# Dense products on plain float32 operands instead of three sweeps over high and low parts, in a two-layer hybrid backbone

## The chip, the cores and the metric

The kernel runs on 1 core of one Trainium2 chip, as one launch. The metric is the device time of that core in microseconds (us); lower is better. Six things work side by side on the core: TensorE's matmuls (PE in the rows) and its weight loads (PEld), VectorE (DVE), ScalarE (ACT), GpSimd (POOL), and SyncE (SP), which here only issues transfers.

## The reference

Two layers run over 256 latent tokens and 256 context tokens of width 1024. Each layer is one wide input projection, three token mixers (Fourier mixing, a gated delta rule, differential attention), three output projections merged under gates, an output projection, and a squared-ReLU MLP. All arrays are float32.

```
u_f, dn_qkv, dn_z, dn_ab, da_q, da_k, da_v, gates = split_columns(h @ w_in)     # 1024 -> 7184
y_f  = fourier_mix(u_f) @ w_f
y_dn = deltanet_output(o_dn, dn_z, dn_gain, h.dtype) @ w_dn
y_da = diff_output(o_da, da_gain, lam_init) @ w_da
y = gated_merge(y_f, y_dn, y_da, gates) @ w_o
x = x + g1 * y
h2 = rms_norm(x, norm2[l]) * (1 + sc2) + sh2
x = x + g2 * squared_relu_mlp(h2, w_mlp1[l], w_mlp2[l])                          # 1024 -> 4096 -> 1024
```

In layer 0 both streams run through everything, so the products are mostly 512 columns (tokens) wide. In layer 1 only the latent tokens go past the mixers, so most products are 256 columns wide.

## The kernel before, in words

Every weight matrix is cut into chunks of 128 x 1024 floats (512 KB). `load_w` brings one chunk into a ring of four buffers called `raw` (a transfer issued by SP), then ScalarE writes a rounded copy `whi` in float32r (a 32-bit type that TensorE takes in one sweep), and VectorE (GpSimd for some chunks) writes the rest, `wlo` = `raw` - `whi`. The moving side is split in the same way: the modulated input `h` into `hh` and `hl`, the MLP's inner activations into two tiles `a`, the mixers' outputs into `yh`/`yl` and `ydh`/`ydl`; `split` does it with one ScalarE copy and one VectorE subtraction.

`mm3` then makes one 128 x 128 block of a product with three matmuls into the same PSUM bank: high x high, low x high, high x low. `gemm` runs the eight blocks of a chunk; `step_of` runs one block of several chunks while the input is still being made (in the fronts of both layers and at the start of each MLP).

A few products take plain float32 operands before and after the change: the 128 x 128 steps of the delta rule (`state`, `k`, `U`, `vn`, ...), attention scores (`km`, `q`) and values (`aT`, `vt`), and the conditioning vector's product with 384 columns (`wn`, `cT`). The levels of a triangular inverse (`Tm`, `Um`, `C`, `X`) run in float16, 64 columns wide.

The order of work on TensorE is set by priorities. Dense products record their own time in `Weave.account`, and the steps of the delta rule and of attention ("chains") are placed between them at times that are given in the same count: `at(t)` looks up which dense product stands at time t. So what `account` believes of a product's length decides how many dense products stand between two steps of a chain.

The first branch's gated results are written out to HBM (`spill`) and read back into `merged` before the other two branches are added; `merged` is then split into `hh`/`hl` for the output projection.

Of the kernel before, what the change touches and what calls it, by code (L numbers as in the profile page):

```python
# [49 lines left out]
LN2 = math.log(2.0)  # L50
FWD = (2, 3, 0, 1)
# [78 lines left out]

SHIFT = ((0, 48), (80, 0))
PAD = {"y": (48, 0), "yd": (40, 104), "a": ((0, 112), (0, 0))}


def pad(pool, w):
    if w:
        pool.tile([P, w], F32, name="pad")


class Weave:  # L140
# [24 lines left out]
    def transpose(self, out, a, ident):  # L165
        self.pe.transpose(out, a, ident)
        self.account(ident, 4)
# [14 lines left out]
def body(tc, A, dbg=None):  # L182
# [13 lines left out]
    hs = [[], []]  # L196
    for t_, at_ in zip(("hh", "hl"), SHIFT):
        t = hp.tile([P, KT * T + max(at_)], F32R, name=t_)
        for l_ in range(DEPTH):
            hs[l_].append(t[:, at_[l_]:at_[l_] + KT * T].rearrange("p (k c) -> p k c", c=T))  # L200
    wx = ExitStack()

    wp = wx.enter_context(tc.tile_pool(name="wp", bufs=3, reuse_waits="tile"))
# [37 lines left out]
    turn_dn = [0]  # L241

    def load_w(l, n, pair=None, eng=V):
        if l == 1 and n < C_U:

            eng = (G, V)[turn_dn[0] % 2]
            turn_dn[0] += 1
        r = raw_tile(A["wck"][l, n])
        if pair is None:
            hi = wp.tile([P, 1024], F32R, tag="whi", name="whi")  # L250
            lo = wp.tile([P, 1024], F32R, tag="wlo", name="wlo")
        else:
            hi, lo = pair[:, 0], pair[:, 1]
# [15 lines left out]
    def step_of(jobs, k, t0, n, order=range(KT), X=hs[0]):  # L269

        for ps, w, m in jobs:
            mm3(ps[0:m, t0:t0 + n], w[0][:, k], w[1][:, k], X[0][:, k, t0:t0 + n], X[1][:, k, t0:t0 + n], k == order[0], k == order[-1])

    def split(src, hi, lo):
        S.copy(hi, src)  # L275
        V.tensor_tensor(out=lo, in0=src, in1=hi.bitcast(F32), op=ALU.subtract)  # L276
# [65 lines left out]
    def lambdas(pool):  # L342
        raw = wp.tile([P, 1024], F32, tag="raw", name="raw", bufs=4)
# [16 lines left out]
    strir = cst.tile([P, 2, P], F32R, name="strir")  # L360
# [4 lines left out]
    def masks():  # L365
# [3 lines left out]
        r = raw_tile(A["kc"][:, K_STRI:K_STRI + 256], 256)  # L369
        S.copy(strir, r.rearrange("p (a b) -> p a b", a=2))  # L370
# [82 lines left out]
    def modulate(l, x, r, a, base, s, k, pool, eng=V):  # L453
        sl = slice(s * L, (s + 1) * L)
        t = pool.tile([P, L], F32, tag="mt", name="mt", bufs=3)
        hi, lo = hs[l][0][:, k, sl], hs[l][1][:, k, sl]
        gain, shift = a[:, k, s:s + 1], ada[l][:, base + k, s:s + 1]
        V.scalar_tensor_tensor(out=t, in0=x[s][:, k], scalar=gain, in1=r[s], op0=ALU.mult, op1=ALU.mult)
        S.activation(hi, t, AF.Identity, bias=shift)
        if eng is V:  # L460
            V.scalar_tensor_tensor(out=lo, in0=t, scalar=shift, in1=hi.bitcast(F32), op0=ALU.add, op1=ALU.subtract)
        else:
            S.activation(t, t, AF.Identity, bias=shift)
            eng.tensor_tensor(out=lo, in0=t, in1=hi.bitcast(F32), op=ALU.subtract)

    def mixer(l, last, front):
# [3 lines left out]
        H = hs[l]  # L470
# [15 lines left out]
        def product(key, c, m, eng=V):  # L486
            return pre.pop(key) if key in pre else gemm(load_w(l, c, None, eng), H, m)

        def gate_weights():
            w = raw_tile(A["wab"][l].rearrange("p a b -> p (a b)"), 128).rearrange("p (a b) -> p a b", b=16)  # L490
            wab = [wp.tile([P, 8, 16], F32R, tag=f"wab{i}", name=f"wab{i}", bufs=1) for i in range(2)]
            split(w, wab[0], wab[1])
            return wab

        def dn_gates():
# [14 lines left out]
            def rest():  # L510
                with weave.chain() as at:
# [27 lines left out]
                    ghr = mk("ghr", F32R)  # L539
                    V.tensor_copy(ghr, g)  # L540
                    glo = mk("glo")
                    V.tensor_tensor(out=glo, in0=g, in1=ghr.bitcast(F32), op=ALU.subtract)
                    glr = mk("glr", F32R)
                    V.tensor_copy(glr, glo)
                    at(t0 + GATE[1])
                    for d in range(2):
                        gd = g[:, d].rearrange("p a b -> p (a b)")
                        PE.matmul(pc[:, 16 * d:16 * d + 16], tri[d], gd, start=True, stop=True)
                        for i, x_ in enumerate((ghr, glr)):
                            PE.matmul(pc[:, 32 + 16 * d:48 + 16 * d], strir[:, d], x_[:, d].rearrange("p a b -> p (a b)"), start=i == 0, stop=i == 1)  # L550
# [7 lines left out]
                    gates.update(beta=beta, ghi=ghr, glo=glo, neg=neg, bend=bend, eg=ee[:, 0], egl=ee[:, 2], g=g)  # L558
# [90 lines left out]
        def dn_chain(p, q2, k2, ktm, vtm, since, lat):  # L649
# [40 lines left out]
            def prepare(steps, t0):  # L690
# [16 lines left out]
                for i, s in enumerate(steps):  # L707
                    tiles = (FWD[s], BWD[s])
                    rh, rl = quad("rh", F32R), quad("rl", F32R)
                    for u, (d, h) in enumerate(units):  # L710
                        for r_, g_ in ((rh, gates["ghi"].bitcast(F32)), (rl, gates["glo"])):
                            g_ = g_[:, d, s, 2 * p + h:2 * p + h + 1]
                            S.activation(r_[:, u], tri[d], AF.Copy, scale=g_)
# [157 lines left out]
        spill = dram.tile([P, KT, n], F32, name=f"spill{l}")  # L871

        early = {}

        def open_gate(cg, i, eng=V):
            ps = product((cg, i), cg + i, n, eng)
# [4 lines left out]
        def branch(cg, cp, Y, put, side, ahead=2):  # L881

            ths, wpj = {i: early.pop((cg, i)) for i in range(KT) if (cg, i) in early}, None
            for i in range(KT + ahead):
# [9 lines left out]
                V.scalar_tensor_tensor(out=th, in0=th, scalar=1.0, in1=pp_[:, :n], op0=ALU.add, op1=ALU.mult)  # L894
                put(j, th)
                side()

        def fnet():
# [4 lines left out]
            ct = [fp.tile([P, 2 * L], F32R, name=f"ct{i}") for i in range(2)]  # L903
            split(raw_tile(A["ct"], 2 * L), ct[0], ct[1])
            ct = [c_.rearrange("p (k c) -> p k c", k=2) for c_ in ct]
            cc = [fp.tile([P, 256], F32R, name=f"cc{i}") for i in range(2)]
            split(raw_tile(A["kc"][:, K_CC:K_CC + 256], 256), cc[0], cc[1])
# [3 lines left out]
            for c in range(4):  # L911
                w = [w_.rearrange("p k c -> p (k c)") for w_ in load_w(l, C_U + c)]
                for i in range(2):
                    k, cols = 2 * c + i, slice(512 * i, 512 * i + 512)
                    for t in range(nt):
                        tk = slice(t * P, (t + 1) * P)
                        mm3(ps[t], H[0][:, k, tk], H[1][:, k, tk], w[0][:, cols], w[1][:, cols], k == 0, k == KT - 1)
            u = [fp.tile([P, nt, 512], F32R, name=f"u{i}") for i in range(2)]
            for t in range(nt):
                split(ps[t], u[0][:, t], u[1][:, t])  # L920
            units = [(g, s) for g in range(4) for s in range(nseq)]

            def positions(i):

                pq = bank("pg").rearrange("p (a c) -> p a c", a=2)
                for j, (g, s) in enumerate(units[i:i + 2]):
                    gs = slice(g * P, (g + 1) * P)
                    for k in range(2):
                        mm3(pq[:, j], u[0][:, 2 * s + k, gs], u[1][:, 2 * s + k, gs], ct[0][:, k], ct[1][:, k], k == 0, k == 1)
                return pq  # L930

            def channels(i, z):

                pa_, pb_ = (abank()[:, :2 * w_].rearrange("p (a c) -> p a c", a=2) for w_ in (NC + 1, NC - 1))
                mm3(pa_, cc[0][:, 0:P], cc[1][:, 0:P], z[0][:, :, 0:NC + 1], z[1][:, :, 0:NC + 1], True, True)
                mm3(pb_, cc[0][:, P:2 * P], cc[1][:, P:2 * P], z[0][:, :, NC - 1:L], z[1][:, :, NC - 1:L], True, True)

                y = fp.tile([P, 2, L], F32, tag="y", name="y")
                sn = y[:, :, L - 1:NC - 1:-1]
                S.copy(y[:, :, NC:L], pb_[:, :, NC - 2:0:-1])  # L940
# [3 lines left out]
                g = units[i][0]  # L944
                hi, lo = (t[:, g:g + 2] if last else t[:, g].rearrange("p (a c) -> p a c", a=2) for t in yb)
                split(y, hi, lo)
# [566 lines left out]
```

## Time and profile before

| | |
|---|---|
| time, median of 3 runs | 1585.76 us (1582.19 to 1586.18) |
| the profiled execution's own time | 1584.71 us |
| its span, first to last instruction | 1582.6 us |
| TensorE matmuls busy | 1517.0 us (96%), 10114 instructions |
| weight loads busy | 1305.2 us (82%) |
| VectorE / ScalarE / GpSimd busy | 1166.3 / 735.4 / 145.0 us |
| moved from and to HBM | 209.42 MB read, 4.20 MB written |

Busy times overlap between engines, and matmuls overlap each other: a matmul of 512 columns is shown with about 0.39 us, while the next one starts well before it ends. How fast TensorE gets through its work is therefore read from the distance between starts, not from durations.

### The profile page before, as it was taken

What the parts mean: (1) busy time and instruction counts of PE and PEld (TensorE: products, weight loads), DVE (VectorE), ACT (ScalarE), POOL (GpSimd) and SP (SyncE); (2) the same over time, 40 slices, a digit from 0 to 9 for tenths busy, and PEclk for the clock granted to TensorE, in tenths of its full rate; (3) what the DMA queues carried; (4) which work ended last, traced back from release to release, by engine and by line L of the source; (5) the groups of instructions that cost most, each with busy time, mean ns of one, the idle gap of its engine ahead of it and who ended that gap; (6) DMA issues with size and microseconds to landing.
All of it is one profiled execution on the core that took longest, in us unless ns stands there. A gap on an engine that the chain in (4) does not pass through costs nothing. (4 is left out here: it accounts for less than half of the span.)

```text
span 1582.6 us, 26109 instructions
## 1 busy us (share of the span) xinstructions
PE 1517.0 (96%) x10114; PEld 1305.2 (82%) x10114; DVE 1166.3 (74%) x2246; ACT 735.4 (46%) x1527; POOL 145.0 (9%) x173
## 2 busy tenths in 40 slices
PE   5899999999999999999999998899999999999997
PEld 2588888777888878888888888888988899999997
DVE  8787774768789797867676755776777886877765
ACT  3475533676532233423223233575457644555543
POOL 3400100011000012000000004001111100100001
PEclk9999999999999999999999999899999999999998
DMA  7532124211257573566566542141332135655662
GB/s 237 192 97 67 35 75 124 82 48 35 80 187 226 189 237 109 164 193 195 181 196 186 186 148 86 56 150 48 111 103 68 42 106 186 188 175 184 190 185 93
DMA packets 64461, 215.31 MB, mean 136 GB/s; under 512 B 7281, under 2 KB 12305, under 8 KB 64081
## 3 DMA queue, kind: packets, MB, share of 16 engines
q1 hardware_dynamic: 58178, 201.96, 40.7%
q10 hardware_dynamic: 5184, 7.21, 1.4%
q0 software_dynamic: 976, 4.48, 1.0%
q8 instruction: 79, 1.29, 0.4%
q14 instruction: 44, 0.36, 0.1%
HBM read 209.42 MB, written 4.20 MB: 135 GB/s over the span
## 5 line engine op out<-in xcount | busy, mean ns | idle before, releaser
L254 ACT CAST whi<-raw 128x1024 fp32r<-128x1024 f32 x277 | 290.5, 1050 | 220.6 <-PE pg L158 98.5
L255 DVE TENSOR_TENSOR wlo<-raw,whi 128x1024 fp32r<-128x1024 f32 x269 | 329.7, 1226 | 80.1 <-ACT whi L254 71.3
L158 PE MATMUL pg<-hh,whi 128*128 128x512 f32 (+1 forms) x856 | 304.0, 355 | 0.2
L158 PE MATMUL pg<-hh,wlo 128*128 128x512 f32 (+1 forms) x856 | 302.9, 354 | 0.5 <-DVE wlo L255 0.5
L158 PE MATMUL pg<-hl,whi 128*128 128x512 f32 (+1 forms) x856 | 303.1, 354 | 0.0
L336 DVE CUSTOM_DVE_ANT_0 junk<-raw,cb 128x1024 f16<-128x1024 f32 x128 | 157.0, 1227 | 57.8 <-DMA raw<-in_wt 56.3
L158 PEld LDWEIGHTS pg<-hh,whi 128*128 128x128 f32 x856 | 162.7, 190 | 20.6 <-issue 0.8
L158 PEld LDWEIGHTS pg<-hl,whi 128*128 128x128 f32 x856 | 162.8, 190 | 19.5 <-issue 0.8
L158 PEld LDWEIGHTS pg<-hh,wlo 128*128 128x128 f32 x856 | 162.7, 190 | 19.1 <-DVE wlo L255 0.7
L158 PE MATMUL pg<-a,whi 128*128 128x256 f32 (+1 forms) x448 | 107.5, 324 | 0.1
L435 POOL TENSOR_TENSOR acc<-acc,sq 128x256 f32<-128x256 f32 x36 | 38.1, 1067 | 661.7 <-ACT sq L433 661.7
L632 DVE SCALAR_TENSOR_TENSOR cy<-cu,conv,cy 128x512 f32<-128x512 f32 (+1 forms) x96 | 69.3, 723 | 30.3 <-ACT cy L630 29.0
L158 PEld LDWEIGHTS pg<-a,whi 128*128 128x128 f32 x448 | 75.8, 188 | 7.7 <-DVE a L276 0.8
L158 PE MATMUL pg<-a,wlo 128*128 128x256 f32 (+1 forms) x224 | 72.1, 322 | 0.0
L878 ACT ACTIVATE gt<-pg 128x256 f32<-128x256 f32 (+1 forms) x43 | 21.0, 488 | 102.6 <-PE pg L158 99.3
L158 PE MATMUL pd<-a,whi 128*128 128x512 f32 (+1 forms) x224 | 56.7, 334 | 0.1
L158 PE MATMUL pa<-hh,whi 128*128 128x512 f32 (+1 forms) x152 | 54.5, 358 | 1.0 <-ACT cy L630 0.9
L158 PE MATMUL pa<-hh,wlo 128*128 128x512 f32 (+1 forms) x152 | 54.0, 355 | 0.0
L158 PE MATMUL pa<-hl,whi 128*128 128x512 f32 (+1 forms) x152 | 53.6, 353 | 0.0
L1235 DVE TENSOR_TENSOR mr<-mr 128x512 f32<-128x512 f32 (+1 forms) x64 | 35.4, 555 | 23.6 <-ACT mr L1234 23.6
L158 PE MATMUL pg<-whi,hh 128*128 128x256 f32 (+1 forms) x160 | 50.9, 318 | 0.7 <-DVE q L996 0.5
L158 PE MATMUL pg<-wlo,hh 128*128 128x256 f32 (+1 forms) x160 | 50.1, 314 | 0.0
(444 smaller groups left out, 3611.4 us busy)
## 6 DMA issues: line engine op xcount, KB each, us to landing
raw<-in_wck SPq DMA_DIRECT2D x280, 512.0 KB, 3.6
raw<-in_wt SPq DMA_DIRECT2D x80, 512.0 KB, 3.6
wv<-in_wt SPq DMA_DIRECT2D x10, 512.0 KB, 4.1
wn<-in_wn SPq DMA_DIRECT2D x16, 192.0 KB, 3.7
x<-in_xin SPq DMA_DIRECT2D x4, 512.0 KB, 8.2
spill<-gt ACTq DMA_DIRECT2D x8, 256.0 KB, 3.9
cb<-crow POOLq DMA_DIRECT2D x2, 1024.0 KB, 7.0
merged<-spill ACTq DMA_DIRECT2D x8, 256.0 KB, 4.6
```

Of the source, the lines that this page charges most:

```text
L158: ins = self.pe.matmul(out, a, b, start=start, stop=stop)
L254: S.copy(hi, r)
L255: eng.tensor_tensor(out=lo, in0=r, in1=hi.bitcast(F32), op=ALU.subtract)
L336: V.tensor_tensor_reduce(out=junk, in0=r, in1=self.cb[:, v], scale=0.5, scalar=0.0, op0=ALU.mult, op1=ALU.add, accum_out=ada[l][:, n, v:v ...
L435: G.tensor_tensor(out=self.acc[s], in0=self.acc[s], in1=q, op=ALU.add)
L632: V.scalar_tensor_tensor(out=y3, in0=u[:, 0:ns, j:j + L], scalar=conv[:, f, j:j + 1], in1=y3, op0=ALU.mult, op1=ALU.add)
L878: S.activation(th, ps[:, :n], AF.Tanh, scale=0.5)
L1235: V.tensor_tensor(out=t, in0=t, in1=t, op=ALU.mult)
```

## The change

Weights are used straight from `raw`, whose ring grows from 4 to 11 buffers; `whi`, `wlo`, `hl`, the second halves of `a`, `y`, `yd` and the Fourier tiles are gone, and with them every copy and subtraction that made them. Each block of a product is one matmul on float32 operands. `merged` becomes a tile that stays in SBUF from the first branch to the output projection, so the transfers of `spill` and the split of `merged` go. `Weave.account` counts a float32 product as 2 sweeps instead of 4 (an ordering number, no work). In the last MLP the appended column count falls from two to one (258 to 257 columns), and two small float32r pairs (`ghr`/`glr`, `rh`/`rl`) become one float32 product each.

```diff
-    wp = wx.enter_context(tc.tile_pool(name="wp", bufs=3, reuse_waits="tile"))
+    wp = wx.enter_context(tc.tile_pool(name="wp", bufs=1, reuse_waits="tile"))
...
-        self.account(b, 4 if b.dtype == F32 else 1)
+        self.account(b, 2 if b.dtype == F32 else 1)
...
+    H = hp.tile([P, KT, T], F32, name="h")
+    M = hp.tile([P, KT, T], F32, name="merged")
...
-        r = wp.tile([P, 1024], F32, tag="raw", name="raw", bufs=4)
+        r = wp.tile([P, 1024], F32, tag="raw", name="raw", bufs=RAW)
...
-    def load_w(l, n, pair=None, eng=V):
...
-        S.copy(hi, r)
-        eng.tensor_tensor(out=lo, in0=r, in1=hi.bitcast(F32), op=ALU.subtract)
-        return hi.rearrange("p (k c) -> p k c", c=P), lo.rearrange("p (k c) -> p k c", c=P)
-
-    def mm3(ps, wh, wl, xh, xl, first, last):
-        PE.matmul(ps, wh, xh, start=first, stop=False)
-        PE.matmul(ps, wl, xh, start=False, stop=False)
-        PE.matmul(ps, wh, xl, start=False, stop=last)
+    def load_w(l, n, dst=None):
+        if dst is None:
+            dst = raw_tile(A["wck"][l, n])
         else:
+            nc.sync.dma_start(dst, A["wck"][l, n])
+        return dst.rearrange("p (k c) -> p k c", c=P)
 
     def gemm(w, X, n, k0=0, kts=KT, t0=0):
         ps = bank()
         for k in range(kts):
-            mm3(ps[:, :n], w[0][:, k0 + k], w[1][:, k0 + k], X[0][:, k, t0:t0 + n], X[1][:, k, t0:t0 + n], k == 0, k == kts - 1)
+            PE.matmul(ps[:, :n], w[:, k0 + k], X[:, k, t0:t0 + n], start=k == 0, stop=k == kts - 1)
...
-        S.activation(hi, t, AF.Identity, bias=shift)
-        if eng is V:
-            V.scalar_tensor_tensor(out=lo, in0=t, scalar=shift, in1=hi.bitcast(F32), op0=ALU.add, op1=ALU.subtract)
-        else:
-            S.activation(t, t, AF.Identity, bias=shift)
-            eng.tensor_tensor(out=lo, in0=t, in1=hi.bitcast(F32), op=ALU.subtract)
+        S.activation(H[:, k, s * L:(s + 1) * L], t, AF.Identity, bias=ada[l][:, base + k, s:s + 1])
...
-                        for j, r_ in enumerate((rh, rl)):
-                            PE.matmul(pD[:, d * 256:(d + 1) * 256], strir[:, d], flat(r_)[:, d * 256:(d + 1) * 256],
-                                      start=False, stop=d == 1 and j == 1)
+                        PE.matmul(pD[:, d * 256:(d + 1) * 256], stri[:, d], flat(r_)[:, d * 256:(d + 1) * 256], start=False, stop=d == 1)
...
+                dst = M[:, j, :n] if first else th
+                V.scalar_tensor_tensor(out=dst, in0=th, scalar=1.0, in1=pp_[:, :n], op0=ALU.add, op1=ALU.mult)
+                if not first:
+                    V.tensor_tensor(out=M[:, j, :n], in0=M[:, j, :n], in1=th, op=ALU.add)
...
-        M = tp.tile([P, KT, n], F32, name="merged")
-        for j in range(KT):
-            nc.scalar.dma_start(M[:, j], spill[:, j])
...
-        for k in range(KT):
-            split(M[:, k], H[0][:, k, :n], H[1][:, k, :n])
...
-                V.tensor_tensor(out=t, in0=t, in1=t, op=ALU.mult)
-                split(t, a[0][:, j], a[1][:, j])
+                V.tensor_tensor(out=a[:, j], in0=t, in1=t, op=ALU.mult)
...
-                          lambda: job(("dn", 0, 0), load_w(0, C_DN, None, G), "pg"),
+                          lambda: job(("dn", 0, 0), load_w(0, C_DN), "pg"),
```

How this changes the order is best seen at two places on TensorE. The first is layer 0's MLP, where the first matrix ends and the second begins (`hh`, `hl` and `h` are its input, `a` the inner activations, `pg`, `pa`, ... the PSUM banks; `a_6472` and `a_6474` are the high and the low part). Before:

```order
L158 MATMUL pa<-hh,whi 128x512
L158 MATMUL pa<-hh,wlo 128x512
L158 MATMUL pa<-hl,whi 128x512
L158 MATMUL pg<-a_6472,whi 128x512
L158 MATMUL pg<-a_6472,wlo 128x512
L158 MATMUL pg<-a_6474,whi 128x512
```

Now:

```order
L150 MATMUL pa<-h,raw 128x512 x8
L150 MATMUL pg<-a,raw 128x512 x8
L150 MATMUL pc<-a,raw 128x512 x8
L150 MATMUL pd<-a,raw 128x512 x8
L150 MATMUL pg<-a,raw 128x512 x8
```

Each group of three matmuls has become one, and nothing else stands between them. The second place is the first float16 inverse of layer 0, between the last matmuls of one step (`Tm`, `C`) and the first of the next (`X`, `Um`). Before, eight dense matmuls in a row stand there, three of which make one product:

```order
L158 LDWEIGHTS C_1956
L158 MATMUL pd<-Tm,C_1956 128x64
L158 MATMUL pg<-hh,whi 128x512
L158 MATMUL pg<-hh,wlo 128x512
L158 MATMUL pg<-hl,whi 128x512
L158 MATMUL pa<-z_1295,cc_1046 128x260
L158 MATMUL pa<-z_1295,cc_1047 128x260
L158 MATMUL pa<-z_1296,cc_1046 128x260
L158 MATMUL pg<-hh,whi 128x512
L158 MATMUL pg<-hh,wlo 128x512
L158 LDWEIGHTS Um
L158 MATMUL pd<-X,Um 128x64
```

Now, at a comparable step of the same inverse, whole dense products stand between single matmuls of the step:

```order
L150 LDWEIGHTS C_1252
L150 MATMUL pd<-Tm,C_1252 128x64
L150 MATMUL pg<-h,raw 128x512
L150 LDWEIGHTS C_1252
L150 MATMUL pd<-Tm,C_1252 128x64
L150 MATMUL pg<-h,raw 128x512
L150 LDWEIGHTS C_1252
L150 MATMUL pd<-Tm,C_1252 128x64
L150 MATMUL pg<-h,raw 128x512 x2
L150 LDWEIGHTS Um
L150 MATMUL pd<-X,Um 128x64
```

A step's eight matmuls are now spread between dense products. Over the whole program TensorE leaves a run of these 64-column matmuls for another product 231 times instead of 125.

## Rows read from the trace of the kernel before

**Rows 1.** Head of the page: busy time and share, and TensorE's granted clock in 40 slices.

```profile
span 1582.6 us, 26109 instructions
PE 1517.0 (96%) x10114; PEld 1305.2 (82%) x10114; DVE 1166.3 (74%) x2246; ACT 735.4 (46%) x1527; POOL 145.0 (9%) x173
...
PEclk9999999999999999999999999899999999999998
```

**Rows 2.** Busy us per engine by stretch: layer 0's MLP, layer 1's MLP with the tail.

```profile
640.00:948.00 308.00, 308.00 (x1364) 255.02 (x1363) 215.41 (x315) 94.63 (x126) 1.77 (x2) 1.00 0.59 185
...
1396.00:1583.00 187.00, 175.80 (x1485) 174.39 (x1483) 128.10 (x207) 91.22 (x163) 6.90 (x6) 0.98 0.54 167
```

**Rows 3.** Timeline of TensorE, layer 0's MLP: start, us, instruction, count.

```profile
691.12 0.39 PE L158 MATMUL pg<-a,wlo 128*128 128x512 f32 x1
...
693.16 0.39 PE L158 MATMUL pg<-a,wlo 128*128 128x512 f32 x1
```

**Rows 4.** Chain that ended last, layer 1's MLP: 256 columns, then 258 columns.

```profile
1417.41 2.72 PE pd L158 x24
...
1433.73 2.87 PE pg L158 x24
```

**Rows 5.** Timeline of TensorE, the attention values of layer 0, 256 columns.

```profile
189.67 0.28 PE L158 MATMUL pg<-whi,hl 128*128 128x256 f32 x1
...
190.38 0.28 PE L158 MATMUL pg<-whi,hl 128*128 128x256 f32 x1
```

**Rows 6.** Timeline of TensorE, plain float32 with 384 columns, in the front.

```profile
33.75 2.10 PE L158 MATMUL pd<-wn,cT 128*2 128x384 f32 x6
...
39.40 2.74 PE L158 MATMUL pd<-wn,cT 128*2 128x384 f32 x8
```

**Rows 7.** Timeline of TensorE, plain float32 with 512 columns (attention scores).

```profile
202.59 1.13 PE L158 MATMUL pa<-km,q 64*128 64x512 f32 x4
```

**Rows 8.** Timeline around one step of a float16 inverse, layer 0.

```profile
331.15 0.41 PE L158 MATMUL pd<-X,Um 128*128 128x64 f16 x8
...
331.40 0.47 PE L158 MATMUL pg<-hh,wlo 128*128 128x512 f32 x1
...
331.71 0.40 PE L158 MATMUL pg<-hl,whi 128*128 128x512 f32 x1
...
331.94 0.60 PE L166 MATMUL pa<-kc,pe 128*128 128x128 f32 x4
...
332.75 0.40 PE L158 MATMUL pd<-Tm,C 128*128 128x64 f16 x8
...
333.19 0.69 DVE L745 TENSOR_TENSOR X<-pd,lvl 128x512 f16<-128x512 f32 x1 [0.86 <-PE pd L158]
```

**Rows 9.** Page, costliest groups: the two that make the weights' high and low parts.

```profile
L254 ACT CAST whi<-raw 128x1024 fp32r<-128x1024 f32 x277 | 290.5, 1050 | 220.6 <-PE pg L158 98.5
L255 DVE TENSOR_TENSOR wlo<-raw,whi 128x1024 fp32r<-128x1024 f32 x269 | 329.7, 1226 | 80.1 <-ACT whi L254 71.3
```

**Rows 10.** Waits of TensorE for split operands: us in total, times, longest.

```profile
PE pc L158 <- DVE hl L461: 2.4, 2, 2.1
...
PE pc L158 <- POOL hl L464: 2.1, 3, 0.9
...
PE pg L158 <- DVE wlo L255: 1.8, 2, 1.3
PE pd L158 <- POOL wv L255: 1.1, 1, 1.1
```

**Rows 11.** Timelines of DVE and POOL in the first 31 us.

```profile
9.15 0.69 DVE L1276 TENSOR_TENSOR sq<-sq 128x512 f32<-128x512 f32 x1 [2.96 <-ACT sq L1309]
...
17.98 2.55 DVE L1276 TENSOR_TENSOR tot<-sq 128x256 f32<-128x256 f32 x1
...
20.46 2.82 DVE L1276 TENSOR_TENSOR sq<-sq 128x512 f32<-128x512 f32 x1
...
28.29 2.27 DVE L383 TENSOR_SCALAR rne<-rne 128x4 f32<-128x4 f32 x1
...
16.82 5.92 POOL L255 TENSOR_TENSOR wlo<-raw,whi 128x1024 fp32r<-128x1024 f32 x2 [2.15 <-ACT whi L254]
```

More of the change, by code (lines that the diff above doesn't have):

```diff
@@ L166, in transpose @@
         self.pe.transpose(out, a, ident)
-        self.account(ident, 4)
+        self.account(ident, 2)
     @contextmanager
@@ L265, in gemm, with step_of @@
         for k in range(kts):
-            mm3(ps[:, :n], w[0][:, k0 + k], w[1][:, k0 + k], X[0][:, k, t0:t0 + n], X[1][:, k, t0:t0 + n], k == 0, k == kts - 1)
+            PE.matmul(ps[:, :n], w[:, k0 + k], X[:, k, t0:t0 + n], start=k == 0, stop=k == kts - 1)
         return ps
-    def step_of(jobs, k, t0, n, order=range(KT), X=hs[0]):
+    def step_of(jobs, k, t0, n, order=range(KT), X=H):
         for ps, w, m in jobs:
[L272 to L276, printed above, removed]
+            PE.matmul(ps[0:m, t0:t0 + n], w[:, k], X[:, k, t0:t0 + n], start=k == order[0], stop=k == order[-1])
     cT = cst.tile([P, 8, 2], F32, name="cT")
@@ L484, in job, with product @@
             return pre[key], w, rows
-        def product(key, c, m, eng=V):
-            return pre.pop(key) if key in pre else gemm(load_w(l, c, None, eng), H, m)
+        def product(key, c, m):
+            return pre.pop(key) if key in pre else gemm(load_w(l, c), H, m)
         def gate_weights():
-            w = raw_tile(A["wab"][l].rearrange("p a b -> p (a b)"), 128).rearrange("p (a b) -> p a b", b=16)
-            wab = [wp.tile([P, 8, 16], F32R, tag=f"wab{i}", name=f"wab{i}", bufs=1) for i in range(2)]
-            split(w, wab[0], wab[1])
+            wab = wp.tile([P, 8, 16], F32, tag="wab", name="wab", bufs=1)
+            nc.sync.dma_start(wab, A["wab"][l])
             return wab
@@ L548, in rest @@
                         PE.matmul(pc[:, 16 * d:16 * d + 16], tri[d], gd, start=True, stop=True)
-                        for i, x_ in enumerate((ghr, glr)):
-                            PE.matmul(pc[:, 32 + 16 * d:48 + 16 * d], strir[:, d], x_[:, d].rearrange("p a b -> p (a b)"), start=i == 0, stop=i == 1)
+                        PE.matmul(pc[:, 32 + 16 * d:48 + 16 * d], stri[:, d], gd, start=True, stop=True)
                         PE.matmul(pc[:, 64 + 16 * d:80 + 16 * d], one32, gd, start=True, stop=True)
@@ L869, in dn_chain, with open_gate @@
             weaving.__exit__(None, None, None)
-        spill = dram.tile([P, KT, n], F32, name=f"spill{l}")
         early = {}
-        def open_gate(cg, i, eng=V):
-            ps = product((cg, i), cg + i, n, eng)
+        def open_gate(cg, i):
+            ps = product((cg, i), cg + i, n)
             th = mp.tile([P, n], F32, tag="gt", name="gt", bufs=4)
@@ L879, in open_gate, with branch @@
             return th
-        def branch(cg, cp, Y, put, side, ahead=2):
+        def branch(cg, cp, Y, side, ahead=2, first=False):
             ths, wpj = {i: early.pop((cg, i)) for i in range(KT) if (cg, i) in early}, None
@@ L902, in fnet @@
                 lambdas(fp)
[L903 to L907, printed above, removed]
+            ct = fp.tile([P, 2 * L], F32, name="ct")
+            nc.sync.dma_start(ct, A["ct"])
+            ct = ct.rearrange("p (k c) -> p k c", k=2)
+            cc = fp.tile([P, 256], F32, name="cc")
+            nc.sync.dma_start(cc, A["kc"][:, K_CC:K_CC + 256])
             nt = n // P
@@ L911, in fnet @@
             for c in range(4):
-                w = [w_.rearrange("p k c -> p (k c)") for w_ in load_w(l, C_U + c)]
+                w = load_w(l, C_U + c).rearrange("p k c -> p (k c)")
                 for i in range(2):
@@ L915, in fnet @@
                     for t in range(nt):
-                        tk = slice(t * P, (t + 1) * P)
-                        mm3(ps[t], H[0][:, k, tk], H[1][:, k, tk], w[0][:, cols], w[1][:, cols], k == 0, k == KT - 1)
-            u = [fp.tile([P, nt, 512], F32R, name=f"u{i}") for i in range(2)]
+                        PE.matmul(ps[t], H[:, k, t * P:(t + 1) * P], w[:, cols], start=k == 0, stop=k == KT - 1)
+            u = fp.tile([P, nt, 512], F32, name="u")
             for t in range(nt):
-                split(ps[t], u[0][:, t], u[1][:, t])
+                S.copy(u[:, t], ps[t])
             units = [(g, s) for g in range(4) for s in range(nseq)]
@@ L928, in positions @@
                     for k in range(2):
-                        mm3(pq[:, j], u[0][:, 2 * s + k, gs], u[1][:, 2 * s + k, gs], ct[0][:, k], ct[1][:, k], k == 0, k == 1)
+                        PE.matmul(pq[:, j], u[:, 2 * s + k, gs], ct[:, k], start=k == 0, stop=k == 1)
                 return pq
             def channels(i, z):
[L934 to L938, printed above, removed]
+                pa_, pb_ = (abank()[:, :2 * w_].rearrange("p (a c) -> p a c", a=2) for w_ in (NC, NC - 2))
+                PE.matmul(pa_, cc[:, 0:P], z[:, :, 0:NC], start=True, stop=True)
+                PE.matmul(pb_, cc[:, P:2 * P], z[:, :, NC:L], start=True, stop=True)
+                g = units[i][0]
+                y = yb[:, g:g + 2] if last else yb[:, g].rearrange("p (a c) -> p a c", a=2)
                 sn = y[:, :, L - 1:NC - 1:-1]
-                S.copy(y[:, :, NC:L], pb_[:, :, NC - 2:0:-1])
+                S.copy(y[:, :, NC:L], pb_[:, :, NC - 3::-1])
                 S.copy(y[:, :, 0:NC:NC - 1], pa_[:, :, 0:NC:NC - 1])
@@ L943, in channels @@
                 V.tensor_tensor(out=sn, in0=pa_[:, :, 1:NC - 1], in1=sn, op=ALU.add)
-                g = units[i][0]
-                hi, lo = (t[:, g:g + 2] if last else t[:, g].rearrange("p (a c) -> p a c", a=2) for t in yb)
-                split(y, hi, lo)
             pq = positions(0)
             for i in range(0, len(units), 2):
-                z = [fp.tile([P, 2, L], F32R, tag=f"z{j}", name=f"z{j}") for j in range(2)]
-                split(pq, z[0], z[1])
+                z = fp.tile([P, 2, L], F32, tag="z", name="z", bufs=2)
+                S.copy(z, pq)
                 if i + 2 < len(units):
@@ L975, in values @@
                 for k in range(KT):
-                    wh, wl = (x_[:, k % 4] for x_ in w[k // 4])
                     for tt in range(2):
                         tk = slice((2 * tt + i) * P, (2 * tt + i + 1) * P)
-                        mm3(ps[tt][:, i * 256:(i + 1) * 256], H[0][:, k, tk], H[1][:, k, tk], wh, wl, k == 0, k == KT - 1)
+                        PE.matmul(ps[tt][:, i * 256:(i + 1) * 256], H[:, k, tk], w[k // 4][:, k % 4], start=k == 0, stop=k == KT - 1)
             for tt in range(2):
@@ L1075, in mixer @@
         front(mp, dp, job, gate_weights)
-        show(f"h{l}", H[0].bitcast(F32))
+        show(f"h{l}", H)
         yp = ex.enter_context(tc.tile_pool(name="yp", bufs=1, side="right", reuse_waits="tile"))
-        yb = [yp.tile([P, 4, n], F32R, name=t_) for t_ in ("yh", "yl")]
-        pad(yp, PAD["y"][l])
+        yb = yp.tile([P, 4, n], F32, name="yb")
         conv = mp.tile([P, 12, 5], F32, name="conv")
@@ L1100, in mixer @@
         pa_banks(f"pa{l}", 1)
-        show(f"mixed{l}", yb[0].bitcast(F32))
+        show(f"mixed{l}", yb)
         at_ = attention_pool()
@@ L1104, in mixer @@
         values(0, at_[0])
-        branch(C_GF, C_PF, yb, lambda j, th: nc.scalar.dma_start(spill[:, j], th), side)
+        branch(C_GF, C_PF, yb, side, first=True)
         attention(0, qk, *at_)
@@ L1130, in mixer @@
         tp = ex.enter_context(tc.tile_pool(name="tp", bufs=1, reuse_waits="tile"))
-        pad(tp, PAD["yd"][l])
-        yd = [tp.tile([P, 4, n], F32R, name=t_) for t_ in ("ydh", "ydl")]
+        yd = tp.tile([P, 4, n], F32, name="yd")
         for h in range(HEADS):
@@ L1138, in mixer @@
                 PE.transpose(pt[:, t * P:(t + 1) * P], on[:, t], ident)
-            V.scalar_tensor_tensor(out=zs[h], in0=pt[:, :n], scalar=gain, in1=zs[h], op0=ALU.mult, op1=ALU.mult)
-            split(zs[h], yd[0][:, h], yd[1][:, h])
-        M = tp.tile([P, KT, n], F32, name="merged")
-        for j in range(KT):
-            nc.scalar.dma_start(M[:, j], spill[:, j])
+            V.scalar_tensor_tensor(out=yd[:, h], in0=pt[:, :n], scalar=gain, in1=zs[h], op0=ALU.mult, op1=ALU.mult)
         if l == 0:
             aw = Rows([(0, i, 2) for i in range(16, 40)], cond_rows(tp), tp)
-        def merge(j, th):
-            V.tensor_tensor(out=M[:, j], in0=M[:, j], in1=th, op=ALU.add)
-        branch(C_GD, C_PD, yd, merge, side, 3)
-        branch(C_GA, C_PA, yb, merge, side)
+        branch(C_GD, C_PD, yd, side, 3)
+        branch(C_GA, C_PA, yb, side)
         ax.close()
@@ L1189, in __init__ @@
             mod_gain(l, S_N2, 24, self.a)
[L1190 to L1193 removed]
+            self.h = pool.tile([P, KT, L + 1], F32, name="gh")
+            S.copy(self.h[:, :, L:L + 1], ada[l][:, 24:32, 0:1])
         def add(self, s, k):
[L1196 to L1198 removed]
+            V.tensor_scalar(out=self.h[:, k, 0:L], in0=self.x[s][:, k], scalar1=self.a[:, k, 0:1], scalar2=None, op0=ALU.mult)
             self.norm.add(s, k)
```

94 lines of the change are left out of this document (24 added, 70 removed).

## The prediction

> **What bounds the kernel now.** I read the head of the page first: TensorE's matmuls are busy 96% of the span and its clock is granted in full almost everywhere [rows 1]. A busy share alone says little, because matmuls overlap, so the next view is the table of stretches. In layer 0's MLP TensorE is busy 308.00 of 308.00 us, VectorE 215.41 and ScalarE 94.63 [rows 2]: nothing there waits for anyone but TensorE. Then the distances between starts. In that stretch three products, nine matmuls of 512 columns, go from 691.12 to 693.16 [rows 3]: 2.04 us, 0.68 us a product, 0.227 us a sweep, with no gap between them. In layer 1's MLP 24 sweeps take 2.72 us at 256 columns and 2.87 us at 258 [rows 4], which is 0.113 and 0.120 a sweep; in the mixers it is (190.38 - 189.67) / 6 = 0.118 us at 256 columns [rows 5]. So the end is set by the number of sweeps on TensorE and by what one takes. The 290.5 us of ScalarE and 329.7 us of VectorE that make the high and low parts [rows 9] lie beside it.
>
> **What a float32 product costs.** This is the term that decides. The program before has 7372 float32r, 1344 float16, 262 transpose and 568 plain float32 matmuls, 9546 together; the page counts 10114 [rows 1], exactly 568 more. So a float32 matmul runs as two instructions. What one of the two takes is read from the conditioning products: eight of them last 2.74 us, six 2.10 us [rows 6], so two more cost 0.64, and one costs 0.32 us for 384 columns, 0.833 ns a column. A float32r sweep costs 0.227 / 512 = 0.443 ns a column. Half of a float32 product is thus not one sweep but nearly two. The two halves together cost 0.853 us at 512 columns, 0.427 at 256, 0.428 at 257.
>
> Bounds: the wn rows have only two weight columns, and no row shows float32 with 128 x 128 weights and more than 128 moving columns. From above, the attention scores have 512 columns and weights over 64 rows: two products side by side take 1.13 us [rows 7]; less the 0.16 us by which a matmul outlasts the distance to the next (0.39 against 0.227) [rows 3], that is 0.48 us a half, 0.96 a product, with one unhidden weight load in it. From below, a half cannot be shorter than one float32r sweep, 0.227. I take 0.853: the wn rows run in series as dense products do.
>
> The row gives 0.833 ns a column, twice. The Trainium skill, "FP8 and Floating Point Precision", section "TensorE Precision Notes", speaks against the change: true float32 is four passes through the array, high and low of each side against both. Four passes where three stood are a third more; with 0.227 us for each of them a product would be 0.908 us instead of 0.853, and the sum below +405 us instead of +303. The row agrees with four passes and makes each a little cheaper than a float32r sweep.
>
> **The sum.** Products by width, counted in the changed program (and, times three, in the one before): 1128 of 512 columns, 1032 of 256, 256 of 257.
> - 512: 1128 x (0.853 - 0.681) = +194 us.
> - 256: before, 0.34 to 0.355 a product [rows 4, 5], I take 0.345; 1032 x (0.427 - 0.345) = +85.
> - 257: 256 x (0.428 - 0.360) = +17.
> - The delta rule's decay products: 64 sweeps of 0.118 become 32 products of 0.427: +6. The Fourier channel products, 36 sweeps into 12: +1.
> - Together +303 us of TensorE.
>
> What is removed elsewhere hides behind TensorE now, so it is worth only what TensorE waited for it. Those waits are short: 2.4, 2.1, 1.8 and 1.1 us are the largest [rows 10], about 10 with the smaller ones; a product still waits for `h` or `a` itself, so I take -6. In the front, GpSimd's subtractions (5.92 us for two) run beside VectorE, and there the same 128 x 512 addition takes 2.82 us that took 0.69 before; two more operations are stretched alike [rows 11]. They stand ahead of the first dense product: 3 x 2.1 = -6. The `spill` transfers and the split of `merged` end no wait of these sizes: 0.
>
> What is added: after a run of float16 matmuls the next dense matmul cannot hide its weight load. It takes 331.71 - 331.40 = 0.31 us where 0.227 is usual [rows 8]. Such returns go from 125 to 231: 106 x 0.08 = +9. And `account` now believes 0.427 us of a 512-column product that will take 0.853, so fewer products stand between two steps of a chain, at some places only one. A step takes: its eight matmuls 0.25 us (331.15 to 331.40), so they are issued by 333.00; VectorE's X ends at 333.88 [rows 8]; 0.9 us. One product covers 0.853. For 112 inverse levels and 48 state steps that is up to 11 us; I take +5.
>
> Rings of 11 buffers let transfers start earlier. VectorE frees no buffer any more, TensorE does; I price that at 0, since TensorE's own waits for `wlo` are 1.8 us. If that cover went, loads late by 1 us on each of 277 chunks would be 277 us, but the transfer engines are busy 0.59 and 0.54 of their time in the MLPs, which take the weights fastest [rows 2], and the span gets longer.
>
> 1582.6 + 303 - 6 - 6 + 9 + 5 = 1887.6 us of span. The profiled execution took 2.1 us more than its span and lies 1.05 below the median of three: **1890 us**.
>
> **Rivals.**
> - *Float32 halves are single sweeps* (faster, the other side). The mechanism: with all 128 weight columns a half streams at 0.227 us for 512. Then a product is 0.454, 0.23 and 0.24 us at the three widths: 1128 x -0.227 + 1032 x -0.115 + 256 x -0.12 = -405 us, about **1180 us**. It wins from the point where a half at 512 columns costs under 0.34 us. For it: no row of this kernel has that form, and two instructions a product would look the same. Against: both float32 rows, at 0.32 for 384 and 0.48 for 512, are far over.
> - *Four full passes*: each as long as a float32r sweep, 0.227. Then 1128 x 0.227 + 1032 x 0.115 + 256 x 0.12 = +405 us, with the other terms about **2000 us**. The rule named above would lead there; the wn row, at 0.32 and not 0.34 for 384 columns, speaks against it, weakly.
> - *Chains become exposed*: in layer 1 one 256-column product (0.427 us) often stands alone between steps of 0.9 us. 56 levels x 0.5 us + 104 other steps x 0.1 = 38 us instead of 5, about **1925 us**, up to 1960 if the attention steps do the same. For it: the order. Against: steps' own matmuls are spread between products, which lets the first results start early.
> - *No difference* would need every product to cost 0.68: no row near it.
>
> **How the numbers follow.** My forecast 0.80 (1855 to 1925 by itself), exposed chains 0.08, four full passes 0.05, single sweeps 0.06, no difference 0.01. 1845 to 1960 holds the first two and leaves out 0.12. What a measurement of this kernel can tell from no change is about 0.3%, 5 us. Faster by more 0.06, within 0.01, slower 0.93.
>
> **What would show it.** 7686 matmul records, two for each of 3032 float32 products. In layer 0's MLP, starts 0.427 us apart, two a product, and the stretch about 308 x 0.853 / 0.681 = 386 us; layer 1's MLP about 224 instead of 187. ScalarE and VectorE each lose 300 us of work and more, and the span does not follow. The first dense product some 6 us earlier. If starts in the MLP are 0.23 us apart, the first rival is right and I am wrong by all of the sum; if TensorE's idle time is over 110 us, the chains are exposed.

## The result, and the profile after

The changed kernel takes 1876.41 us (median of 4 runs, 1874.2 to 1877.49), the one before 1584.45 (median of 4, 1582.19 to 1586.18): a ratio of 1.184, 95% interval 1.182 to 1.186. The forecast was 1890, range 1845 to 1960, slower. The profiled execution has a span of 1875.4 us and took 1877.21.

First the head of the page, against [rows 1].

```profile
span 1875.4 us, 19979 instructions
PE 1825.3 (97%) x7686; PEld 1119.3 (60%) x7686; DVE 772.9 (41%) x1810; ACT 398.8 (21%) x1058; POOL 83.8 (4%) x146
...
PEclk9999999999999999999999999999999999999999
```

TensorE has 7686 matmul records instead of 10114 and is busy 308 us longer. VectorE lost 393 us of work, ScalarE 337, GpSimd 61, and the span grew by 293. The clock row shows 9 (90% or more) in every slice, and the mean over the span is 0.993 against 0.991 before, so the clock does not explain the +293 us.

The MLPs show the price of a product with nothing beside it. The table of stretches (as [rows 2], with the same work inside each: the stretch, its length, busy us and instructions of PE, PEld, DVE, ACT and POOL, granted clock, DMA share, GB/s) and then TensorE's timeline: start, us, instruction, count.

```profile
754.00:1141.00 387.00, 387.00 (x907) 172.36 (x906) 119.07 (x208) 19.87 (x35) 0.00 (x0) 1.00 0.42 140
1647.00:1875.00 228.00, 217.72 (x1011) 190.46 (x1009) 48.37 (x119) 25.59 (x75) 4.34 (x6) 0.98 0.40 127
```

```profile
899.88 7.03 PE L150 MATMUL pg<-h,raw 128*128 128x512 f32 x16
906.75 1.45 PE L150 MATMUL pc<-a,raw 128*128 128x512 f32 x3
...
1700.12 3.64 PE L150 MATMUL pa<-gh,raw 128*128 128x257 f32 x16
1703.60 3.64 PE L150 MATMUL pg<-gh,raw 128*128 128x257 f32 x16
```

Layer 0's MLP takes 387 us where 308 stood, layer 1's with the tail 228 where 187 stood. Sixteen records of 512 columns go from 899.88 to 906.75: 0.429 us each, 0.858 a float32 product, where three float32r sweeps took 0.681 [rows 3]. At 257 columns a record is 3.48 / 16 = 0.2175 us, 0.435 a product, where 0.36 stood [rows 4].

Last the waits that grew or shrank (TensorE's, us in total, times, longest). After:

```profile
PE pg L150 <- DVE tot L1198: 9.2, 2, 6.7
PE pd L158 <- DVE on L1075: 7.6, 3, 5.1
```

and before:

```profile
PE pg L158 <- DVE tot L1276: 13.5, 2, 11.1
```

The front's wait is 4.4 us shorter (the first dense product starts at 30.99 us instead of 35.77). The wait for `on`, the normalized output of the delta rule, was not among the longest before.

To see all waits at once, I added up the distances between the starts of successive matmuls in each trace, and set apart every place where a distance is over 0.4 us longer than that kind of matmul usually takes. Such long waits are 62.1 us in 50 places before and 48.7 in 42 after, -13. All the rest, the streaming with its small gaps, is 1509.1 before and 1815.5 after, +306. The two make the span's +293.

### The profile page after: what moved, and what is told of

Its sections match the earlier page's. It is cut to its first block, busy times and chain, and to the rows that moved or that the text cites. A ratio compares the mean times of both kernels' runs of the same rounds, so it can differ in the third digit from the quotient of the medians.

```text
span 1875.4 us, 19979 instructions
## 1 busy us (share of the span) xinstructions
PE 1825.3 (97%) x7686; PEld 1119.3 (60%) x7686; DVE 772.9 (41%) x1810; ACT 398.8 (21%) x1058; POOL 83.8 (4%) x146
## 3 DMA queue, kind: packets, MB, share of 16 engines
HBM read 206.28 MB, written 1.06 MB: 111 GB/s over the span
## 4 chain that ended last, share of the span: by engine, by line
PE 90%; DVE 5%; ACT 2%; DMA 1%; issue 1%; POOL 0%; DVEq 0%; ACTq 0%; POOLq 0%
PE pg L150 51%; PE pd L150 14%; PE pa L150 13%; PE pc L150 11%; DVE junk L306 1%; DVE cy L584 1%; PE pc L158 1%; PE pa L158 1%; ACT sw L939 0%; DMA wv<-in_wt 0%; DMA rows<-in_rows 0%; DVE C L671 0%; DMA raw<-in_wt 0%; DVE sq L1198 0%; ACT sjd L380 0%
## 5 line engine op out<-in xcount | busy, mean ns | idle before, releaser
L150 PE MATMUL pg<-h,raw 128*128 128x512 f32 (+1 forms) x1600 | 624.5, 524 | 1.1 <-ACT vt L925 1.1
L150 PEld LDWEIGHTS pg<-h,raw 128*128 128x128 f32 x1600 | 283.9, 192 | 199.6 <-issue 185.1
L150 PE MATMUL pg<-a,raw 128*128 128x256 f32 (+1 forms) x448 | 139.0, 463 | 0.0
L150 PEld LDWEIGHTS pg<-a,raw 128*128 128x128 f32 x448 | 85.1, 190 | 49.3 <-issue 42.5
L150 PE MATMUL pg<-raw,h 128*128 128x256 f32 (+1 forms) x320 | 99.8, 437 | 0.7 <-ACT km L942 0.6
L150 PE MATMUL pg<-yb,raw 128*128 128x512 f32 (+1 forms) x256 | 94.2, 493 | 0.2 <-ACT vt L925 0.2
L150 PE MATMUL pa<-h,raw 128*128 128x512 f32 (+1 forms) x224 | 90.0, 548 | 0.0
L150 PE MATMUL pd<-a,raw 128*128 128x512 f32 (+1 forms) x224 | 74.5, 486 | 0.0
L150 PE MATMUL pa<-a,raw 128*128 128x256 f32 (+1 forms) x208 | 64.2, 462 | 0.0
L150 PE MATMUL pc<-a,raw 128*128 128x512 f32 (+1 forms) x192 | 63.9, 486 | 0.0
```

## Experiments

All were compared with the kernel before on the same chip. Differences to the kernel before go by the ratio, those to the changed kernel by the medians (two chips were used, on which the kernel before took 1585.28 to 1585.42 us).

**The changed kernel again.**

> The changed kernel as it is, so that its three variants run beside it on the same chip: 1876 us, within 3.

Measured: 1877.19 us, ratio 1.1846 (1.1827 to 1.1866). The variants of the order, of the ring and of the removed work are compared with this.

**One product, by itself.** Layer 0's second MLP matrix on plain float32, in the kernel before:

```diff
+    def load_raw(l, n):
+        return [raw_tile(A["wck"][l, n]).rearrange("p (k c) -> p k c", c=P)]
...
+            if len(X) == 1:
+                PE.matmul(ps[:, :n], w[0][:, k0 + k], X[0][:, k, t0:t0 + n], start=k == 0, stop=k == kts - 1)
+                continue
...
+                if plain:
+                    V.tensor_tensor(out=a[0][:, j], in0=t, in1=t, op=ALU.mult)
```

> The kernel before, with only layer 0's second MLP matrix on plain float32: 232 products of 512 columns and 48 of 256, without parts of these weights and of `a`. Theory 1 (the cost lies in the products, each by itself): 232 x (0.858 - 0.681) + 48 x (0.432 - 0.345) = +45 us, 1629 (1625 to 1633). Theory 3 (the parts that are no longer made give something back): 1620 or less. If the cost lay in the order or in the chains of the mixers, which this leaves alone, nothing: 1584.

Measured: 1628.29 us, ratio 1.0273 (1.0257 to 1.0289): +43 us, 41 to 46. The price lies in the products, and it adds up: the 232 are a fifth of the 512-column products, in a stretch where TensorE waits for nothing, and there the work on parts that is gone gives nothing back that can be measured.

**The order.** The changed kernel, with `account` counting four units for a float32 operand and for a transpose, as it did before the change:

```diff
-        self.account(b, 2 if b.dtype == F32 else 1)
+        self.account(b, 4 if b.dtype == F32 else 1)
...
-        self.account(ident, 2)
+        self.account(ident, 4)
```

> The changed kernel, but the order counts four units for a float32 product, so that 0.853 us is believed of a 512-column product instead of 0.427. Theory 1 (the end is set by TensorE's columns, and one product covers a step of a chain): within 4 us of the changed kernel, at most the 5 us of the prediction's chain term less, 1871 to 1879. Theory 2 (the time depends on how many products the order puts between the steps of a chain): over 8 us away, faster if steps were exposed, slower if work for cover now runs out before the chains end.

Measured: 1852.99 us, ratio 1.1698 (1.1679 to 1.1718), 24 us faster. Theory 2 holds here, and theory 1, mine, does not. The delta rule's first pair shows why. VectorE's `on`, its last step (first and last start among the numbers), in the changed kernel:

```profile
L1075 DVE TENSOR_TENSOR on<-oD,rD x8: 415/554/686, 527.8 to 1545.0; 128x512 f32<-128x512 f32 x4, 128x256 f32<-128x256 f32 x4
```

and with four units:

```profile
L1075 DVE TENSOR_TENSOR on<-oD,rD x8: 415/551/684, 464.7 to 1514.3; 128x512 f32<-128x512 f32 x4, 128x256 f32<-128x256 f32 x4
```

and, in its waits, what is left of TensorE's 7.6 us for `on`:

```profile
PE pd L158 <- DVE on L1075: 0.4, 1, 0.4
```

A step is placed at a time of the count. Where the count believes half of what a product takes, more products stand ahead of each step, the chain is drawn out (its end moves from 464.7 to 527.8 us), and when the products run out its last steps stand bare. With four units TensorE's long waits are 30.8 us instead of 48.7. That is 18 of the 25 us by which this profile's span is shorter. The rest goes with the clock: its mean is 0.998 instead of 0.993, and between 500 and 560 us, where the chain's end stands bare in the changed kernel, it is 0.94 there and 1.00 with four units.

**The order, in the kernel before.** All believed lengths halved there too:

```diff
-        self.account(b, 4 if b.dtype == F32 else 1)
+        self.account(b, 2 if b.dtype == F32 else 0.5)
...
-        self.account(ident, 4)
+        self.account(ident, 2)
```

> The kernel before, with all lengths that the order believes halved: half a unit for a float32r sweep, two for a plain float32 matmul and for a transpose. No work changes. If a halved count by itself stretches the chains over twice as many products and leaves their ends bare, as the changed kernel's order did (24 us there): slower by 15 to 40 us, 1600 to 1625. If it costs only where a product is one float32 matmul: 1585 within 4.

Measured: 1696.18 us, ratio 1.0706 (1.0687 to 1.0724): +112 us, far beyond what I expected in the direction that I expected. TensorE's timeline at the end of that chain, then the stretch around it and two of the matmul groups by themselves:

```profile
481.50 0.39 PE L158 MATMUL pd<-X,Um 128*128 128x64 f16 x8 [1.09 <-DVE X L745]
482.67 0.41 PE L158 MATMUL pd<-id,Tm 128*128 128x64 f16 x8 [0.79 <-DVE Tm L754]
...
494.83 1.92 PE L158 MATMUL pc<-state,q 128*128 128x128 f32 x8
...
503.08 1.06 PE L158 MATMUL pc<-state,q 128*128 128x128 f32 x8
505.96 0.33 PE L166 MATMUL pd<-kc,on 128*128 128x128 f32 x1 [1.82 <-DVE on L1135]
```

```profile
450.00:550.00 100.00, 76.56 (x471) 60.42 (x470) 70.46 (x145) 24.79 (x59) 2.14 (x2) 0.83 0.34 109
494.83:496.75 1.92, 1.92 (x10) 1.92 (x10) 0.00 (x0) 0.65 (x2) 0.00 (x0) 0.50 0.00 0
503.08:504.14 1.06, 1.06 (x10) 0.87 (x8) 0.76 (x2) 0.00 (x0) 0.27 (x1) 1.00 0.00 0
```

Here not the last steps but some 25 us of steps stand without a product between them. TensorE, busy 76.56% of that stretch, is granted 0.83 of its clock on the mean. The same eight matmuls take 1.92 us at 494.83, at 0.50 (the level of 1.2 GHz), and 1.06 at 503.08, at 1.00 (2.4 GHz). Long waits and slower matmuls make up this run together: added up as above, long waits are 65 us longer than before, and all the rest is 45 us longer, with the same matmuls and a mean clock of 0.962 instead of 0.991.

**The ring.** The changed kernel with 4 buffers (`RAW = 4` instead of 11):

> The changed kernel with 4 buffers in the ring of loaded weights instead of 11. Theory 1: a 512-column chunk lasts 6.9 us on TensorE, so four of them hold 27 us of work ahead, and the time stays within 4 us of the changed kernel, 1873 to 1880. Theory 2 (the 12 us that the change cost less than forecast come from loads that start earlier): 1884 or more.

Measured: 1869.16 us, ratio 1.1803 (1.1782 to 1.1824), 8 us faster than the changed kernel; neither theory had a gain. The timeline around the delta rule's second `on`, in the changed kernel:

```profile
541.94 0.16 DVE L816 TENSOR_TENSOR rD<-roy,rq 128x8 f32<-128x8 f32 x1
542.05 1.22 DVE L306 CUSTOM_DVE_ANT_0 junk<-raw,cb 128x1024 f16<-128x1024 f32 x1
543.21 0.08 DVE L306 DVE_READ_ACCUMULATOR2_ANT ada<- 128x1 f32 x1
543.21 1.29 DVE L1075 TENSOR_TENSOR on<-oD,rD 128x512 f32<-128x512 f32 x2
544.04 1.94 PE L158 MATMUL pd<-kc,on 128*128 128x128 f32 x8 [5.12 <-DVE on L1075]
```

and with 4 buffers:

```profile
535.99 0.17 DVE L816 TENSOR_TENSOR rD<-roy,rq 128x8 f32<-128x8 f32 x1
536.19 1.29 DVE L1075 TENSOR_TENSOR on<-oD,rD 128x512 f32<-128x512 f32 x2
...
538.29 1.04 PE L158 MATMUL pd<-kc,on 128*128 128x128 f32 x8
```

The conditioning rows of the next layer (`junk`, 1.22 us each on VectorE) come through the same ring as the weights. In the changed kernel nine of them stand among the small steps that lead to `on`, one after nearly each step of 0.16 us; with 4 buffers there are four. TensorE's wait of 5.12 us goes. The stretch around that place, first in the changed kernel, then with 4 buffers:

```profile
528.00:550.00 22.00, 15.69 (x40) 7.29 (x40) 20.23 (x42) 3.64 (x18) 0.00 (x0) 0.86 0.60 209
528.00:550.00 22.00, 19.59 (x52) 8.69 (x51) 17.10 (x37) 2.66 (x12) 0.00 (x0) 1.00 0.51 160
```

The granted clock is 0.86 there in the changed kernel and 1.00 with 4 buffers, and the eight matmuls behind `on` take 1.94 and 1.04 us.

**Order and ring together.**

> The changed kernel with both: four units for a float32 product in the order (24 us faster by itself) and a ring of 4 buffers (8 us faster by itself). If the ring's 8 us come from the bare end of the delta rule's first chain, where the conditioning products of a fuller ring stood ahead of `on` on VectorE (543.21 against 536.19 us), the order's change has already covered that place, and the sum is 1850 to 1856. If the two are independent: 1845.

Measured: 1850.61 us, ratio 1.1679 (1.1661 to 1.1697). That is 2.4 us under the order alone, with intervals that overlap: the two are not independent. The ring's cost needs the bare end. This is the change as it would be without its order and its ring, +266 us.

**The removed work, put back.** In the changed kernel, on tiles that nothing reads (ring of 9):

```diff
+            hi = wp.tile([P, 1024], F32R, tag="whi", name="whi", bufs=1)
+            lo = wp.tile([P, 1024], F32R, tag="wlo", name="wlo", bufs=1)
+            S.copy(hi, dst)
+            V.tensor_tensor(out=lo, in0=dst, in1=hi.bitcast(F32), op=ALU.subtract)
```

> The changed kernel with ScalarE's copy (1.05 us each) and VectorE's subtraction (1.23 us each) of every loaded weight chunk put back, into tiles that nothing reads; the ring has 9 buffers and one pair of such tiles. VectorE's busy time goes from 773 to about 1100 us, ScalarE's from 399 to about 690. Theory 1 (this work lies beside TensorE): within 10 us of the changed kernel, 1873 to 1886. Theory 3 (taking it away gave a real gain, which the dearer products hid): 1900 or more, since TensorE's waits beside its products would be back from 108 to 155 us.

Measured: 1905.17 us, ratio 1.2024 (1.1999 to 1.2048), +28. By its number theory 3. But ScalarE waited long for the loads, in its queue (its waits over the whole span), and in layer 0's MLP TensorE waits for activations that are late behind that (TensorE's waits there):

```profile
ACT whi L235 <- DMA raw<-in_wck: 613.1, 212, 9.4
```

```profile
PE pd L150 <- DVE a L1162: 3.2, 1, 3.2
PE pc L150 <- DVE a L1162: 1.8, 1, 1.8
```

The kernel before has no such wait in its MLP [rows 2]: there the copies waited for TensorE to free a pair of tiles [rows 9]. So the same work on scratch tiles, which waits for neither (ring of 8):

```diff
+            S.copy(gcopy, gsrc)
+            V.tensor_tensor(out=gdiff, in0=gsrc, in1=gsrc, op=ALU.subtract)
```

> The changed kernel with the same work put back for each loaded weight chunk, a ScalarE copy and a VectorE subtraction of 128x1024, but on scratch tiles, so that it waits neither for the load nor for the other engine; the ring has 8 buffers. In the run with the work bound to the loads ScalarE stood 613 us waiting for them, and it took 28 us more than the changed kernel. If the waits in the two queues made those 28 us: 1874 to 1884 here. If the busy time itself made them (ScalarE and VectorE late for the chains): 1895 or more.

Measured: 1904.9 us, ratio 1.2019 (1.2 to 1.2037), +28 again, but at another place. The 40 slices of VectorE and ScalarE:

```profile
DVE  9999999999999544433333331253564662222112
ACT  8999999973320001200000001233324430011101
```

With nothing to wait for, the work ran ahead into the first third, where the chains need both engines. Layer 0's MLP begins 25 us late (its first `mr` at 780.5 us instead of 755.4), 25 of the 27 us that this profile's span is longer. In the run above it began 3 us late, and 21 were lost behind that: 7 in this MLP, 11 in layer 1 ahead of its MLP and 3 in the rest. The waits for `a` shown above are thus only a part of that run's loss. So the work costs 28 us where it meets the chains and as much where it waits for loads; it is not free, but neither run says what it cost where the kernel before had it. Both runs also have a smaller ring than the changed kernel, which by itself can gain up to the 8 us found above.

**GpSimd's part.** The kernel before, with the front's subtractions on VectorE; first those of five weight chunks alone, then the activations' too (`load_w(0, C_DN, None, G)` becomes `V`, and `modulate(0, xv, r_, ma, 0, s, k, st, G)` likewise).

> The same with only the five weight subtractions moved to VectorE; the 16 of activations stay on GpSimd. It takes away the two long GpSimd operations (5.92 us for two) that stood beside the stretched VectorE ones. Term of the front right: 1577 to 1582. Otherwise 1584 within 3.

Measured: 1580.74 us, ratio 0.9965 (0.9952 to 0.9978), -5.5.

> The kernel before, with the front's subtractions, five of weights and 16 of activations, on VectorE instead of GpSimd. If the stretching of VectorE beside GpSimd (0.69 to 2.82 us, three places) costs the front 6 us as forecast, and VectorE takes its 1.2 us each off the path: 1576 to 1582. If VectorE is itself the front's bound there: 1584 or slower, by up to 5.

Measured: 1578.53 us, ratio 0.9953 (0.9939 to 0.9967), -7.5. The front's term was right in place and size: TensorE's longest wait for `tot` falls from 11.1 to 6.8 us, close to the changed kernel's 6.7. Then layer 1's subtractions as well:

```diff
-            eng = (G, V)[turn_dn[0] % 2]
+            eng = V
```

> The kernel before with the front's subtractions on VectorE (7 us faster by itself) and, besides, those of layer 1's first 24 weight chunks, every second of which is on GpSimd. If GpSimd stretches VectorE beside it there as in the front: 1570 to 1577. If layer 1's subtractions lie beside TensorE's work and VectorE has no room for more: 1578 or up to 10 more.

Measured: 1569.47 us, ratio 0.9906 (0.9892 to 0.9919), -15. This beats both kernels. (GpSimd had six of these subtractions there, half of 12 chunks, not of 24 as I wrote.) The busy times, and TensorE's longest wait:

```profile
PE 1514.4 (97%) x10114; PEld 1304.2 (83%) x10114; DVE 1161.5 (74%) x2273; ACT 730.2 (47%) x1511; POOL 101.6 (6%) x146
```

```profile
PE pg L158 <- DVE tot L1276: 8.7, 2, 6.8
```

VectorE takes over 27 more operations and is busy 5 us less. Long waits are 48.4 us, 14 fewer than before. For layer 1 no run separates GpSimd's stretching of VectorE from its own slower subtractions.

**Two sweeps instead of three.** The kernel before, `mm3` without its third matmul:

```diff
-        PE.matmul(ps, wl, xh, start=False, stop=False)
-        PE.matmul(ps, wh, xl, start=False, stop=last)
+        PE.matmul(ps, wl, xh, start=False, stop=last)
```

> The kernel before without the third product (high weights by low activations); the low activations are still made, and nothing reads them. It shows what is left when TensorE has a third less to do, as it would by the rival of single sweeps: TensorE's work falls by about 405 us. If nothing else binds: 1180 us. Theory 1 expects VectorE, with 1166 us of work, to bind where the parts are made: 1230 to 1330 us. So the parts are free only beside three sweeps.

Measured: 1376.39 us, ratio 0.8687 (0.8671 to 0.8703), over both my numbers. Busy times, then TensorE's waits:

```profile
PE 1186.2 (86%) x7686; PEld 987.2 (72%) x7686; DVE 1146.6 (83%) x2246; ACT 734.4 (53%) x1527; POOL 148.1 (11%) x173
```

```profile
PE pd L166 <- DVE on L1134: 15.3, 3, 12.0
PE pg L158 <- DVE tot L1275: 15.0, 2, 11.1
PE pd L158 <- DVE Tm L753: 10.6, 15, 2.0
```

By the count of sweeps TensorE has some 405 us less to stream, and only 208 come out. VectorE is not full (83%): TensorE waits for it in the front and at steps of the chains, which two sweeps no longer cover. Added up as above, long waits are 151 us longer than before, and all the rest is 355 us shorter instead of 405, at a mean clock of 0.935 instead of 0.991. Whether the rival with cheap products would have reached its 1180 us in this order is not shown: this run still makes all the parts, which the rival would not.

## Why the prediction was right, and which terms were not

**What bounds the kernel, and the product's price: right.** The wn rows [rows 6] gave 0.833 ns a column a half, 0.427 us at 512 columns; 0.429 was measured, and 7686 records, as counted. The forecast's prices give the run with one matrix, 232 x 0.172 + 48 x 0.082 = +44 us (measured +43). Streaming with its small gaps grew by 306 us against 303 + 9. The rule of four passes (the Trainium skill, "FP8 and Floating Point Precision", "TensorE Precision Notes") fits, if a pass is 0.858 / 4 = 0.2145 us; four times a float32r sweep's 0.227 was too much.

**Returns from float16 runs (+9): right in price, incomplete.** TensorE's timeline, the first dense matmuls behind one float16 matmul:

```profile
495.06 1.11 PE L150 MATMUL pg<-h,raw 128*128 128x512 f32 x2
496.00 0.38 PE L158 MATMUL pa<-kc,pe 128*128 128x128 f32 x2
```

The two halves take 0.94 us instead of 0.858, 0.08 more, as estimated. What I missed is the other edge: the last 512-column float32r sweep ahead of a plain float32 matmul of a chain took 0.074 us more than usual (9.4 us over 127 places in the trace before), the last float32 half takes hardly more in the trace after (nothing on the median of some 150 places). A weight load of 0.19 us fits beside 0.429 and hardly beside 0.227; that this is the reason was not tried by itself.

**Removed work hides (-6 and -6): mis-sized.** The front's -6 held (-7.5 at most by experiment, first product 4.8 us earlier). The -6 for split operands was read from the few waits that name them [rows 10]. With order and ring undone, long waits fell from 62.1 to 28.9 us, -33 instead of -12. In the kernel before, moving GpSimd's subtractions alone takes away some 14, half of them in layer 1, where I had looked for none: work that is late on an engine shows as a wait for something else, as for `tot` in the front. How the rest of the -33 divides is open. The removed work can be one cause; the product itself, which at 0.858 us instead of 0.681 covers more of a chain's step, can be the other. No run has the one without the other, and the two that put the work back moved it to other places.

**Steps of the chains (+5) and the ring (0): the step that failed.** "So fewer products stand between two steps" had the sign wrong: a halved count puts more products ahead of each step. The cost is not one product failing to cover a step, it is a chain drawn out until nothing covers its end. The sum was off as well: 160 steps of 0.9 us against 0.853 are 7.5 us and not up to 11. Order and ring together cost 27 us (1877.19 against 1850.61): 20 are long waits (48.7 against 28.9), and the rest goes with the clock (0.993 against 0.998), which the forecast left out. So the forecast came within 14 us in part because two terms were off in opposite directions: the order and the ring cost 22 us more than I gave them, and without them long waits fell by some 21 us more than I gave the removed work. That these two came out nearly equal is luck.

**Transfers: right.** No wait for a load shows in the MLPs, and the ring of 4 cost nothing there.

**Rivals.** Single sweeps are refuted by 0.429 us a half. Four full passes by 0.858 against 0.908. Exposed chains were real, at 24 us and not 38, by another mechanism (above all the bare end of the delta rule's first chain, in layer 0, and not single products between steps in layer 1), and hidden in the sum by the other error.

## What to carry to other kernels

Price a new operand type per column from any instruction of that type that streams in series, however small, and count its records: here two columns of weights foretold a 128-column product within 1%. When lengths change, look up every number that an order believes of them; halving it cost 24 us in one kernel and 112 in the other, with no work changed. Work on an engine that is not the bound is free only where it meets no chain; the gain of 15 us in the kernel before came from moving work off the idlest engine onto a busier one.

## What the hardware showed unexpectedly

- Two float32 halves of 512 columns take 0.858 us, three float32r sweeps 0.681: the ratio is 1.26. A float32r sweep takes 0.443 ns a column, a float32 half 0.838.
- GpSimd's subtraction of 128x1024 took 2.3 to 3.0 us, VectorE's 1.23; beside GpSimd, VectorE's addition of 128x512 took 2.82 us [rows 11], and 0.69 with the subtraction on VectorE.
- Around a chain without products between its steps, TensorE's mean granted clock was 0.83 over 100 us, and the same eight matmuls took 1.92 us at a granted clock of 0.50 and 1.06 us at 1.00, 8 us later. Such a wait was paid twice: once as idle time, once as slower matmuls.
